# Putting VectorE's sums and low parts of the weights in program order, and moving two waits at the ends

## The chip, the cores and the metric

One core of a Trainium2 chip runs the whole kernel. The metric is the device time of one execution in microseconds (us), lower is better. Engines are named as in the profile: PE is TensorE, DVE VectorE, ACT ScalarE, POOL GpSimd, SP SyncE.

## The reference

One layer of a hybrid decoder trunk, in float32, for 256 tokens of width 2048:

```python
h = x + 0.5 * swiglu(rmsnorm(h, ffn1_norm), ffn1_w_gu, ffn1_w_down)       # D_FF = 5632
proj = rmsnorm(h, mix_norm) @ w_in
gu, gv, z, xbc, dt_raw = jnp.split(proj, split_at, axis=-1)
a_out = chunked_sgu(gelu(gu), gelu(gv), gm_v_norm, gm_w_s, gm_b_s)
m_out = mamba2_group(z, xbc, dt_raw, ssm_conv_w, ssm_conv_b, ssm_dt_bias, ssm_a_log, ssm_d, ssm_norm)
h = h + concatenate([a_out, m_out]) @ w_out
h = h + memory_cross_attention(rmsnorm(h, xa_norm), rmsnorm(mem, mem_norm), xa_w_q, xa_w_kv, xa_w_o)
h = h + 0.5 * swiglu(rmsnorm(h, ffn2_norm), ffn2_w_gu, ffn2_w_down)
return rmsnorm(h, final_norm)
```

Nearly all of the work is in the projections, whose weights are read once from memory.

## The kernel before

Each float32 matrix product is made of three products of parts: every operand is split into a high part in PE's fast float32 format and a low part, which is the rest, and PE adds high x high, high x low and low x high. A weight arrives as a raw block of 128 x 2048 elements (four pieces of 128 x 512; pool `wraw`, 3 buffers). ACT casts it to the high part (`high`, L161; `whigh`, 3 buffers) and DVE subtracts to get the low part (`low`, L166; `wlow`, 2 buffers).

In `proj_sum` there are two kinds of blocks, named by a letter in a string of kinds. A C block is used as it is: 24 matmuls. An S block serves a scheme that saves one of eight products by working on sums of the four pieces: `split_sums` has DVE make four sums in three instructions (L184 two at once, L185, L186), and then the high and low part of three raw pieces and of the four sums: 21 matmuls. The sums and their parts have one buffer each. Products m1, m6, m5 and m7 collect over all S blocks of a group and are read out after the last of them (`mid`), when that block's other products are still to come.

A feed-forward network runs over 11 chunks of 512 hidden columns (kinds CSCSCSCC each, numbered 0 to 10 here), and its down projection comes in two parts, after chunks 4 and 10. Between chunks, the finished hidden chunk is transposed by PE and split into operands: L339 and L340 for operands of C blocks, L410 to L422 (`forms`, `hids`) for those of S blocks. `part` instructions (L496, L523) read PE's results.

The order of instructions on PE is that of the program. On the other engines a scheduler sets the order when the kernel is built, from its own estimate of times. It keeps data dependencies, and it keeps one instruction behind another where the program says so with `behind` (L152). Each engine then runs its queue in that order. Before the change, the sums and low parts of weights are free of such ties, so a low part can stand between two sums or ahead of another block's.

At the end, each of the four column groups `h[0]` to `h[3]` is 128 x 512 for each of two token tiles (t = 0, 1). `finish` (L1016) has ACT square and sum them (L319, output `junk`), DVE and POOL make the reciprocal root (`rstd_of`: L325, L326, L327), and DVE (L1029) and ACT (L1031) scale and store.

## Time and profile before

| | |
|---|---|
| runs (3) | 2515.29, 2517.97 (median), 2519.0 us |
| profiled execution | 2517.8 us, its span 2516.1 us |
| granted PE clock, mean | 0.996 |
| PE busy | 98% of the span |
| DVE busy | 78% |
| ACT busy | 51% |
| POOL busy | 1% |
| memory traffic | 189 GB/s over the span |

A row of the timeline is: start in us, length in us, engine, line, operation, output and inputs, shape, how many in a row, and in brackets the idle time of the engine just before it and what ended that. A row of the windows gives a stretch, its length, busy time and number of instructions of PE, of PE's weight loads, of DVE, ACT and POOL, then the granted PE clock, the share of the DMA engines and GB/s. All times are from the start of the span.

### The profile page before, as it was taken

The page shows a single profiled execution, that of the slowest core. Times are in us where ns is not written, and L with a number is a line of the kernel's source. Part 1 is how long each engine was busy: PE and PEld are TensorE (multiplying, and loading weights), DVE is VectorE, ACT ScalarE, POOL GpSimd, SP SyncE. Part 2 cuts the span into 40 slices and gives each one's busy share as a digit, 9 for nine tenths or more (in the row PEclk, how much of TensorE's full clock was granted, in tenths as well). Part 3 has the DMA queues.
Part 4 walks back from the last instruction along what each step waited for, and adds up shares of the span by engine and source line. Part 5 has one row for each costly group of instructions (what it writes and reads, how often), then busy time and mean ns, then how long its engine had stood idle before and what let it go on. Part 6 is the DMA issues. An engine that isn't in the chain of part 4 may idle for free.

```text
span 2516.1 us, 31418 instructions
## 1 busy us (share of the span) xinstructions
PE 2478.2 (98%) x12673; PEld 2110.1 (84%) x12673; DVE 1951.9 (78%) x1830; ACT 1286.9 (51%) x1164; POOL 21.9 (1%) x46
## 2 busy tenths in 40 slices
PE   9999999999999999999999999999999999999997
PEld 7778888888789998788888999988877888888876
DVE  7888888898776678655688755678798888989876
ACT  6555445555446454435555544455555454555543
POOL 0000000000000000000000000000000000000000
PEclk9999999999999999999999999999999999999999
DMA  7555666555555555545556654555655566566553
GB/s 237 187 197 192 202 209 200 189 197 191 177 175 166 196 179 198 201 159 192 178 191 201 218 173 163 169 183 170 199 191 194 186 200 216 185 201 201 190 195 134
DMA packets 205762, 476.75 MB, mean 189 GB/s; under 512 B 15040, under 2 KB 17248, under 8 KB 204848
## 3 DMA queue, kind: packets, MB, share of 16 engines
q1 hardware_dynamic: 202800, 464.31, 56.1%
q0 software_dynamic: 1840, 9.26, 1.1%
q8 instruction: 99, 1.62, 0.3%
q10 hardware_dynamic: 976, 1.18, 0.1%
q14 instruction: 47, 0.39, 0.0%
HBM read 472.57 MB, written 2.13 MB: 189 GB/s over the span
## 4 chain that ended last, share of the span: by engine, by line
PE 69%; DVE 16%; issue 8%; ACT 4%; DMA 3%; SPq 0%; DVEq 0%; POOL 0%; ACTq 0%; POOLq 0%
PE acc L73 65%; DVE lo L166 8%; ACT hi L161 3%; DVE sum L184 2%; PE tpose L76 1%; DMA raw<-in_w_gu 1%; DVE sum L185 1%; DVE part L496 1%; DMA raw<-in_w_dn 1%; DVE sum L186 1%; PE yp L73 1%; DVE part L523 1%; DVE hids L422 0%; PE logits L73 0%; PE o L73 0%
## 5 line engine op out<-in xcount | busy, mean ns | idle before, releaser
L161 ACT CAST hi<-raw 128x2048 fp32r<-128x2048 f32 (+1 forms) x438 | 791.3, 1807 | 813.9 <-PE acc L73 657.6
L166 DVE TENSOR_TENSOR lo<-raw,hi 128x2048 fp32r<-128x2048 f32 (+1 forms) x438 | 943.6, 2155 | 256.4 <-PE acc L73 190.1
L73 PE MATMUL acc<-hi,xp_ffn 128*128 128x512 f32 x1824 | 577.7, 391 | 1.3 <-ACT hi L176 1.3
L73 PEld LDWEIGHTS acc<-hi,xp_ffn 128*128 128x128 f32 x1824 | 343.5, 188 | 73.1 <-ACT hi L176 2.1
L166 DVE TENSOR_TENSOR lo<-sum,hi 128x2048 fp32r<-128x2048 f32 x109 | 249.6, 2290 | 153.4 <-ACT hi L161 153.4
L73 PE MATMUL acc<-lo,xp_ffn 128*128 128x512 f32 x912 | 356.1, 390 | 0.0
L161 ACT CAST hi<-sum 128x2048 fp32r<-128x2048 f32 x109 | 208.3, 1911 | 210.7 <-DVE sum L186 198.1
L73 PE MATMUL acc<-hi,hid 128*128 128x512 f32 x896 | 282.9, 390 | 0.0
L73 PE MATMUL acc<-hi,xt_mix 128*128 128x512 f32 x768 | 241.9, 393 | 0.0
L73 PEld LDWEIGHTS acc<-lo,xp_ffn 128*128 128x128 f32 x912 | 171.8, 188 | 35.8 <-DVE lo L177 0.4
L73 PEld LDWEIGHTS acc<-hi,hid 128*128 128x128 f32 x896 | 168.3, 188 | 34.8
L73 PE MATMUL acc<-xt_mix,hi 128*128 128x256 f32 x1024 | 186.0, 284 | 0.0
L73 PE MATMUL acc<-lo,hid 128*128 128x512 f32 x448 | 174.5, 390 | 0.0
L73 PEld LDWEIGHTS acc<-hi,xt_mix 128*128 128x128 f32 x768 | 144.3, 188 | 30.3 <-issue 0.5
L496 DVE TENSOR_TENSOR part<-acc,part 128x512 f32<-128x512 f32 x240 | 159.7, 686 | 11.0 <-PE acc L73 3.9
L73 PEld LDWEIGHTS acc<-xt_mix,hi 128*128 128x128 f32 x1024 | 159.8, 192 | 0.3
L73 PE MATMUL acc<-hi,xp_ffn1s 128*128 128x512 f32 x466 | 151.2, 393 | 2.2 <-DVE xp_ffn L340 1.3
L73 PE MATMUL acc<-hi,xp_ffn2s 128*128 128x512 f32 x466 | 150.9, 393 | 1.6 <-DVE hid L340 1.3
L73 PE MATMUL acc<-lo,xt_mix 128*128 128x512 f32 x384 | 149.8, 390 | 0.1
L73 PE MATMUL acc<-xt_mix,lo 128*128 128x256 f32 x512 | 145.5, 284 | 0.7 <-DVE lo L166 0.7
L184 DVE TENSOR_TENSOR sum<-raw 128x1024 f32<-128x1024 f32 x109 | 133.1, 1222 | 8.7 <-DMA raw<-in_w_gu 6.0
L73 PE MATMUL acc<-hi,hids 128*128 128x512 f32 x392 | 130.1, 402 | 0.1
(281 smaller groups left out, 3418.1 us busy)
## 6 DMA issues: line engine op xcount, KB each, us to landing
raw<-in_w_gu SPq DMA_DIRECT2D x286, 512.0 KB, 4.0
raw<-in_w_in SPq DMA_DIRECT2D x80, 1024.0 KB, 5.1
raw<-in_w_dn SPq DMA_DIRECT2D x60, 1024.0 KB, 5.4
raw<-in_w_gu SPq DMA_DIRECT2D x132, 256.0 KB, 4.1
raw<-in_w_kv SPq DMA_DIRECT2D x28, 1024.0 KB, 5.3
raw<-in_w_out SPq DMA_DIRECT2D x21, 1024.0 KB, 5.6
raw<-in_w_q SPq DMA_DIRECT2D x16, 1024.0 KB, 5.2
raw<-in_w_dn SPq DMA_DIRECT2D x28, 512.0 KB, 4.1
```

The costliest lines, as they stand in the source:

```text
L73: return pe(nc.tensor.matmul(out, lhsT=lhsT, rhs=rhs, start=start, stop=stop))
L76: return pe(nc.tensor.transpose(out=out, in_=in_, identity=identity))
L161: nc.scalar.copy(out=t[:, :n], in_=x[:, :n])
L166: nc.vector.tensor_tensor(out=t[:, :n], in0=x[:, :n], in1=hi[:, :n].bitcast(F32), op=ALU.subtract)
L184: nc.vector.tensor_tensor(out=t[:, 0:2], in0=raw[:, 0:3:2], in1=raw[:, 3:4].broadcast_to([P, 2, NC]), op=ALU.add)
L185: nc.vector.tensor_tensor(out=t[:, 2], in0=t[:, 0], in1=raw[:, 2], op=ALU.add)
L186: nc.vector.tensor_tensor(out=t[:, 3], in0=t[:, 2], in1=raw[:, 1], op=ALU.add)
L496: nc.vector.tensor_tensor(out=out, in0=a, in1=b, op=op)
L523: nc.vector.scalar_tensor_tensor(out=g, in0=u, scalar=nrm.rstd[:, t:t + 1], in1=g, op0=ALU.mult, op1=ALU.mult)
```

## The change

Three parts. First, every sum and every low part of a weight goes through `split_op`, which ties it behind the one before it in the program: for an S block the three sums, the low part of the raw pieces, the low part of the sums, and then the next block. Second, the negation of a small constant row (`ex<-rowb`, which needs the load of `rowb`) is tied behind the instruction that makes `dt` in the middle of the kernel. Third, in `finish`, groups 2 and 3 of token tile 0 are multiplied by the final weight ahead (L1032 after the change), what is left of their scaling becomes a product with one scalar (L1048), and that is tied behind the last addition into `h[3]` of tile 1; the order of the four groups is written out anew.

```diff
+    last_split = []
+    def split_op(**kw):
+        with behind(last_split):
+            last_split[:] = [nc.vector.tensor_tensor(**kw).ins]
...
     def low(pool, x, hi, n):
         t = pool.tile([P, 2 * KP, NC], F32R, name="lo")
-        nc.vector.tensor_tensor(out=t[:, :n], in0=x[:, :n], in1=hi[:, :n].bitcast(F32), op=ALU.subtract)
+        split_op(out=t[:, :n], in0=x[:, :n], in1=hi[:, :n].bitcast(F32), op=ALU.subtract)
...
     def split_sums(raw):
         t = wsum.tile([P, 4, NC], F32, name="sum")
-        nc.vector.tensor_tensor(out=t[:, 0:2], in0=raw[:, 0:3:2], in1=raw[:, 3:4].broadcast_to([P, 2, NC]), op=ALU.add)
-        nc.vector.tensor_tensor(out=t[:, 2], in0=t[:, 0], in1=raw[:, 2], op=ALU.add)
-        nc.vector.tensor_tensor(out=t[:, 3], in0=t[:, 2], in1=raw[:, 1], op=ALU.add)
+        split_op(out=t[:, 0:2], in0=raw[:, 0:3:2], in1=raw[:, 3:4].broadcast_to([P, 2, NC]), op=ALU.add)
+        split_op(out=t[:, 2], in0=t[:, 0], in1=raw[:, 2], op=ALU.add)
+        split_op(out=t[:, 3], in0=t[:, 2], in1=raw[:, 1], op=ALU.add)
...
-            nc.vector.scalar_tensor_tensor(out=dt[:, t, :], in0=pdt[:, t, :HEADS], scalar=rstd[:, t:t + 1],
+            raw_ins = nc.vector.scalar_tensor_tensor(out=dt[:, t, :], in0=pdt[:, t, :HEADS], scalar=rstd[:, t:t + 1],
                                            in1=rowb[:, 0, :], op0=ALU.mult, op1=ALU.add)
...
-        nc.vector.tensor_scalar(out=ex[:, NT, :], in0=rowb[:, 1, :], scalar1=-1.0, scalar2=None, op0=ALU.mult)
+        with behind([raw_ins.ins]):
+            nc.vector.tensor_scalar(out=ex[:, NT, :], in0=rowb[:, 1, :], scalar1=-1.0, scalar2=None, op0=ALU.mult)
...
+    scale_first = []
+    def finish(n, t, added):
...
-        if n < 2:
+        if n < 2 or t == 0:
             nc.vector.tensor_tensor(out=h[n][:, t, :], in0=h[n][:, t, :], in1=fws[n], op=ALU.mult)
         if n < 3:
             return
+        if t:
+            with behind([added.ins]):
+                scale_first.pop()()
         r = rstd_of(ss_f[:, t:t + 1, :], f"f{t}")
-        for m in (3, 0, 2, 1):
+        def scale(m):
             o = h[m][:, t, :]
-            if m > 1:
+            if m < 2:
+                nc.scalar.mul(o, o, r)
+            elif t:
                 nc.vector.scalar_tensor_tensor(out=o, in0=o, scalar=r, in1=fws[m], op0=ALU.mult, op1=ALU.mult)
             else:
-                nc.scalar.mul(o, o, r)
+                nc.vector.tensor_scalar(out=o, in0=o, scalar1=r, scalar2=None, op0=ALU.mult)
             queue = nc.sync if m > 1 else nc.scalar if t else nc.gpsimd
             queue.dma_start(out=o_v[:, t, m * NC:(m + 1) * NC], in_=o)
+        for m in (0, 1):
+            if t:
+                scale(3 - m)
+            scale(m)
+        if not t:
+            scale_first.append(lambda: (scale(3), scale(2)))
```

The instructions of SP and POOL keep their order, and so do PE's. What moves is DVE's order, and a little of ACT's. Lines after the change are 7 higher in the stretch of `proj_sum` and the networks; all split operations of weights are recorded at L169.

DVE at the passage from chunk 2 to chunk 3 of the first network, before (the numbers tell buffers apart; sum_1229 belongs to the S block after the C block of lo_1171, hid_1217 to the hidden chunk just made):

```order
L496 TENSOR_TENSOR part_1081<-acc_944,part_1080 128x512
L184 TENSOR_TENSOR sum_1229<-raw_1225 128x1024
L185 TENSOR_TENSOR sum_1229<-sum_1229,raw_1225 128x512
L186 TENSOR_TENSOR sum_1229<-sum_1229,raw_1225 128x512
L166 TENSOR_TENSOR lo_1171<-raw_1166,hi_1169 128x2048
```

and further on, up to L340:

```order
L166 TENSOR_TENSOR lo_1235<-raw_1225,hi_1233 128x1536
L523 SCALAR_TENSOR_TENSOR part_1079<-part_1081,rstd_ffn1_440,part_1079 128x512
L184 TENSOR_TENSOR sum_1301<-raw_1297 128x1024
L166 TENSOR_TENSOR lo_1271<-raw_1266,hi_1269 128x2048
L417 TENSOR_TENSOR forms_1209<-forms_1207 128x256
L422 TENSOR_TENSOR hids_1201<-forms_1207,hids_1201 128x512
L418 TENSOR_TENSOR forms_1209<-forms_1207,forms_1209 128x128
L340 TENSOR_TENSOR hid_1217<-tpose_1218,hid_1217 128x2x256
```

The first of these places on DVE after the change:

```order
L503 TENSOR_TENSOR part_1081<-acc_944,part_1080 128x512
L169 TENSOR_TENSOR lo_1171<-raw_1166,hi_1169 128x2048
L503 TENSOR_TENSOR part_1078<-acc_859,part_1078 128x512
L169 TENSOR_TENSOR sum_1229<-raw_1225 128x1024
L503 TENSOR_TENSOR part_1080<-acc_866,part_1080 128x512
L503 TENSOR_TENSOR part_1079<-acc_873,part_1079 128x512
L530 SCALAR_TENSOR_TENSOR part_1078<-part_1080,rstd_ffn1_440,part_1078 128x512
L503 TENSOR_TENSOR part_1081<-acc_880,part_1081 128x512
L169 TENSOR_TENSOR sum_1229<-sum_1229,raw_1225 128x512
L530 SCALAR_TENSOR_TENSOR part_1079<-part_1081,rstd_ffn1_440,part_1079 128x512
L169 TENSOR_TENSOR sum_1229<-sum_1229,raw_1225 128x512
L169 TENSOR_TENSOR lo_1235<-raw_1225,hi_1233 128x1536
```

and, right behind that, up to the line that was L340 (now L347):

```order
L169 TENSOR_TENSOR lo_1239<-sum_1229,hi_1237 128x2048
L169 TENSOR_TENSOR lo_1271<-raw_1266,hi_1269 128x2048
L424 TENSOR_TENSOR forms_1209<-forms_1207 128x256
L429 TENSOR_TENSOR hids_1201<-forms_1207,hids_1201 128x512
L425 TENSOR_TENSOR forms_1209<-forms_1207,forms_1209 128x128
L347 TENSOR_TENSOR hid_1217<-tpose_1218,hid_1217 128x2x256
```

The three sums of the S block have moved from ahead of lo_1171 to behind it, and the first sum of the next S block (sum_1301) from ahead of lo_1271 to behind L347.

DVE at the last S block of the first down projection, before (its block is raw_4639; raw_4688 is the C block after it):

```order
L184 TENSOR_TENSOR sum_4643<-raw_4639 128x1024
L166 TENSOR_TENSOR lo_4649<-raw_4639,hi_4647 128x1536
L185 TENSOR_TENSOR sum_4643<-sum_4643,raw_4639 128x512
L186 TENSOR_TENSOR sum_4643<-sum_4643,raw_4639 128x512
L166 TENSOR_TENSOR lo_4692<-raw_4688,hi_4690 128x2048
L166 TENSOR_TENSOR lo_4653<-sum_4643,hi_4651 128x2048
```

and there after:

```order
L169 TENSOR_TENSOR sum_4643<-raw_4639 128x1024
L169 TENSOR_TENSOR sum_4643<-sum_4643,raw_4639 128x512 x2
L169 TENSOR_TENSOR lo_4649<-raw_4639,hi_4647 128x1536
L169 TENSOR_TENSOR lo_4653<-sum_4643,hi_4651 128x2048
L169 TENSOR_TENSOR lo_4692<-raw_4688,hi_4690 128x2048
```

The sums stand together, and the low part of the sums ahead of that of the next C block.

DVE at the end of the kernel after the change (h2 and h3 are the column groups, acc PE's results, fw the final weight):

```order
L464 SCALAR_TENSOR_TENSOR h2_92<-acc_18611,h2_92 128x512
L332 TENSOR_REDUCE ms_19000<-ss_f_14000 128x1
L1032 TENSOR_TENSOR h3_93<-h3_93,fw_18994 128x512
L333 TENSOR_SCALAR ms_19000<-ms_19000 128x1
L464 SCALAR_TENSOR_TENSOR h3_93<-acc_18618,h3_93 128x512
L1048 TENSOR_SCALAR h3_93<-h3_93,rstd_f0_18999 128x512
L1048 TENSOR_SCALAR h2_92<-h2_92,rstd_f0_18999 128x512
```

Before, the two scalings of h3 and h2 (L1029) stood right behind the line that is L333 now, ahead of the last addition into h3, and no product of h3 stood between the two steps of the reciprocal root.

## The prediction

> **What bounds the kernel now.** I read the page's first section, then what TensorE (PE) waited for, then the single waits in PE's timeline, the granted clock after them, and VectorE's (DVE) timeline ahead of each kind.

> ```profile
> span 2516.1 us, 31418 instructions
> PE 2478.2 (98%) x12673; PEld 2110.1 (84%) x12673; DVE 1951.9 (78%) x1830; ACT 1286.9 (51%) x1164; POOL 21.9 (1%) x46
> ...
> PE acc L73 <- DVE lo L166: 19.8, 19, 3.5
> PE acc L73 <- DVE hid L340: 2.2, 6, 0.7
> PE acc L73 <- DVE xp_ffn L340: 1.6, 2, 1.3
> ```

> PE is busy for 98% of the span, and its order is the same in both kernels. So the change can win only what PE waits, what PE loses at a lower clock, and the two ends of the span. Of the waits (us in total, times, longest), 19 for a low part are 19.8 us, and 8 for L340, which empties a transpose bank, are 3.8. The waits one by one (in brackets the idle time and what ended it):

> ```profile
> 68.44 0.50 PE L73 MATMUL acc<-hi,xp_ffn1s 128*128 128x512 f32 x1 [1.26 <-DVE xp_ffn L340]
> ...
> 88.19 0.51 PE L73 MATMUL acc<-lo,xp_ffn1s 128*128 128x512 f32 x1 [0.85 <-DVE lo L166]
> ...
> 157.06 0.50 PE L73 MATMUL acc<-hi,xp_ffn1s 128*128 128x512 f32 x1 [0.24 <-DVE hid L340]
> ...
> 643.08 0.79 PE L73 MATMUL acc<-lo,hids 128*128 128x512 f32 x1 [3.51 <-DVE lo L166]
> ...
> 1306.83 0.50 PE L73 MATMUL acc<-lo,mts 128*128 128x512 f32 x1 [1.50 <-DVE lo L166]
> ...
> 1392.75 0.50 PE L73 MATMUL acc<-lo,mts 128*128 128x512 f32 x1 [0.83 <-DVE lo L166]
> ...
> 2268.14 0.51 PE L73 MATMUL acc<-lo,xp_ffn2s 128*128 128x512 f32 x1 [0.48 <-DVE lo L166]
> ...
> 2483.84 0.51 PE L73 MATMUL acc<-lo,hids 128*128 128x512 f32 x1 [3.51 <-DVE lo L166]
> ```

> Four kinds. The down projection's last S block: three waits of 3.51 (643.08, 2415.63 and 2483.84). w_out: 1.50 and 0.83. The last S block of a feed-forward (FFN) chunk: eleven waits, the first 0.85 at 88.19, the last 0.48 at 2268.14, 6.2 together. The remaining three low-part waits, 0.7, lie in the down projections. L340's lie at the passage from one chunk to the next. A matmul that ends a wait lasts 0.50 and delays the next, so a wait costs about 0.15 more than its bracket.

> The clock after the waits (PE's busy time, its granted clock after "PEclk" at the end, as windows):

> ```profile
> 643.08:648.60 5.52, 5.52 (x13) 4.37 (x14) 3.63 (x6) 0.00 (x0) 0.00 (x0) 0.50 0.40 154
> 2416.71:2420.12 3.41, 3.41 (x10) 2.63 (x9) 2.62 (x5) 0.00 (x0) 0.00 (x0) 0.50 0.33 127
> 2484.97:2488.38 3.41, 3.41 (x10) 2.64 (x9) 2.65 (x5) 0.00 (x0) 0.00 (x0) 0.50 0.02 5
> 1308.30:1311.70 3.40, 3.40 (x16) 2.81 (x15) 3.40 (x5) 1.30 (x1) 0.00 (x0) 1.00 0.45 131
> ```

> After each wait of 3.51 PE runs at clock 0.50 for 5.5 or 3.4 us; after the wait of 1.50 it keeps 1.00. In 3.41 us 10 matmuls ran where 16 or 17 would have. The loss is between 10/17 kept (1.4, 1.4 and 2.3, so 5.1) and half (6.2); I take 5.7.

> **The change, part by part.**

> *Down projection.* DVE around the first long wait:

> ```profile
> 633.62 1.75 DVE L166 TENSOR_TENSOR lo<-raw,hi 128x1536 fp32r<-128x1536 f32 x1
> 635.29 0.69 DVE L185 TENSOR_TENSOR sum<-sum,raw 128x512 f32<-128x512 f32 x1
> 636.01 0.69 DVE L186 TENSOR_TENSOR sum<-sum,raw 128x512 f32<-128x512 f32 x1
> 638.53 2.29 DVE L166 TENSOR_TENSOR lo<-raw,hi 128x2048 fp32r<-128x2048 f32 x1 [1.82 <-PE acc L73]
> 640.74 2.29 DVE L166 TENSOR_TENSOR lo<-sum,hi 128x2048 fp32r<-128x2048 f32 x1
> ```

> Two things are late: the sums stand behind a low part (1.67 from start to start), and lo<-sum, which PE needs, stands behind the low part of the next C block, which itself waits for a buffer until 638.53. Chained, lo<-sum runs 2.2 earlier for the second reason and 1.7 for the first, so it ends about 3.9 before 643.03, ahead of the 639.5 at which PE runs dry. The low part put behind it is for the block after this one, a whole S block away, so it has cover. All three waits go (3 x (3.51 + 0.15) = 11.0), the slow clock with them (5.7), and the three small ones (0.7 + 0.45 = 1.1): -17.8. If only the order of the two low parts helped, 1.3 of each wait would stay.

> *w_out.* The same pair (the low part between L184 and L185) makes the two waits there: 1.50 + 0.83 + 0.3, -2.6.

> *Last S block of a chunk.* Here too lo<-sum moves ahead of a low part: 6.2 + 11 x 0.15, -7.9. *First passage of each FFN* (68.44 and its like in the second): L340 comes ahead of a 2.2-us low part, 1.6 + 0.3, -1.9.

> *The other passages between chunks* lose. The one near 141, for DVE, PE and ScalarE (ACT) in turn:

> ```profile
> 139.46 1.23 DVE L184 TENSOR_TENSOR sum<-raw 128x1024 f32<-128x1024 f32 x1 [0.50 <-DMA raw<-in_w_gu]
> ...
> 142.05 2.29 DVE L166 TENSOR_TENSOR lo<-raw,hi 128x2048 fp32r<-128x2048 f32 x1
> ...
> 151.84 1.23 DVE L184 TENSOR_TENSOR sum<-raw 128x1024 f32<-128x1024 f32 x1
> 152.98 2.29 DVE L166 TENSOR_TENSOR lo<-raw,hi 128x2048 fp32r<-128x2048 f32 x1
> ...
> 156.32 0.69 DVE L340 TENSOR_TENSOR hid<-tpose,hid 128x512 fp32r<-128x512 f32 x1
> ...
> 141.03 0.39 PE L73 MATMUL acc<-lo,xp_ffn 128*128 128x512 f32 x1
> ...
> 143.12 1.90 ACT L161 CAST hi<-sum 128x2048 fp32r<-128x2048 f32 x1
> ```

> The low part at 142.05 (lo_1171) writes one of two buffers, which PE leaves with its matmul of 141.03, so at about 141.5. Before, DVE used the time up to then for the block's sums, 139.46 to 142.05. Now lo_1171 stands first in the chain, so DVE waits for 141.5 with the sums queued behind it, and they are done in the stretch that leads to L340, which PE waits for at 157.06. From the end of L340 in before, 157.01: start 0.5 earlier; plus the three sums, 1.14 + 0.60 + 0.60 = 2.34 from start to start; less the next block's L184, which moves behind L340, 1.14; plus 0.4, because lo<-sum now follows its cast closely (cast 1.90 beside a low part of 1.67, and the hand-over). That is 158.1, or 1.1 later, on top of the 0.24 that PE waits there already. Eight passages in each FFN have this order (chunks 2 to 4 and 6 to 10). Where L340 was not waited for, it had little room; I price all sixteen alike, 16 x 1.08 = +17.3. Bounds: 0.4 each (the hand-over alone, the rest covered) and 2.2 (nothing credited for L184): +6 to +35. I take 1.08, since each addend is a duration of this trace. The waits become 1.1 to 1.6 us long, in the class of the 1.50 that kept the clock.

> [...]

> *Opening.* DVE, ACT and PE, and two windows:

> ```profile
> 7.68 0.18 DVE L652 TENSOR_SCALAR ex<-rowb 128x32 f32<-128x32 f32 x1 [6.45 <-DMA rowb<-in_rows]
> 7.78 0.48 DVE L346 SCALAR_TENSOR_TENSOR xp_ffn<-tpose,col,xp_ffn 128x256 fp32r<-128x256 f32 x1
> ...
> 6.30 0.47 ACT L345 ACTIVATE xp_ffn<-tpose,col 128x256 fp32r<-128x256 f32 x1 [2.48 <-PE tpose L76]
> ...
> 9.32 0.79 PE L73 MATMUL acc<-hi,xp_ffn 128*128 128x512 f32 x1 [1.35 <-ACT hi L176]
> ...
> 10.31:13.72 3.41, 3.41 (x9) 2.64 (x10) 1.49 (x3) 0.52 (x1) 0.00 (x0) 1.00 0.99 346
> 13.73:17.14 3.41, 3.41 (x19) 2.81 (x18) 1.06 (x3) 1.58 (x4) 0.00 (x0) 1.00 1.01 342
> ```

> Without L652 ahead, L346 can follow ACT's 6.30 + 0.47 at about 6.82 and not at 7.78; ACT's casts and the first matmul follow: -0.9. Bounds: 0 (the weight loads come late instead) and -2.6 (PE, which runs 9 matmuls in the window before 13.7 and 19 in the next, also comes to its full rate one window sooner: 1.7 more). The moved L652 is 0.18 in a stage where DVE has room: nothing.

> *End.* DVE, then ACT, then PE's last matmul:

> ```profile
> 2506.28 1.42 DVE L1029 SCALAR_TENSOR_TENSOR h<-h,rstd_f,fw 128x512 f32<-128x512 f32 x2 [0.69 <-POOL rstd_f L327]
> 2507.61 0.69 DVE L457 SCALAR_TENSOR_TENSOR h<-acc,h 128x512 f32<-128x512 f32 x1
> ...
> 2506.28 1.33 ACT L1031 ACTIVATE h<-h,rstd_f 128x512 f32<-128x512 f32 x2 [0.18 <-POOL rstd_f L327]
> 2508.33 0.63 ACT L319 ACTIVATE junk<-h 128x512 f32<-128x512 f32 x1 [0.71 <-DVE h L457]
> ...
> 2505.58 0.39 PE L73 MATMUL acc<-hi,hid 128*128 128x512 f32 x1
> ```

> PE's last matmul ends at about 2506.0, and the last addition (2507.61) need no longer wait behind two L1029. But one of the new products stands between L325 and L326, 0.6, so POOL's rstd is that much later, and so are ACT's two scalings, which stay ahead of the last junk: 2506.28 + 0.6 + 1.33 = 2508.2 against 2508.33. Of 1.6 on DVE 0.1 to 0.2 is left: -0.2, between 0 and -1.6.

> Sum: -17.8 - 2.6 - 7.9 - 1.9 + 17.3 - 0.9 - 0.2 = -14.0. The profiled execution took 2517.8 (1.7 beside its span), the median 2517.97, so 2503.8 by the one and 2504.0 by the other.

> **Rivals.**

> *The clock falls at the passages (slower).* Sixteen waits of 1.1 to 1.6 us each followed by 3.41 us at 0.50: 16 x 1.6 = +26, so 2530. For it: nothing here shows a wait between 1.50 and 3.51, and sixteen tries are many. Against: 1.26 and 1.50 without a fall. It decides once nine of sixteen fall.

> *The passages cost their upper bound.* 2.2 each, +35 in place of +17: 2522, within the noise. For it: from 142.05 to L340 every DVE instruction of the rows above follows without idle, so nothing absorbs a further delay, a late weight load for one. Against: the L184 moved behind L340 is seen in the order.

> *The passages cost nearly nothing.* 0.4 each: 2493. For it: PE waits for the banks only, and DVE has 22% of idle time. Against: none of that idle time lies behind lo_1171.

> *The chain doesn't cure the late low parts.* Raw buffers are released later by later low parts, the loads land later, and lo<-sum in the down projections stays late by 2 to 3 us: about 12 of the 17.8 don't come, 2516. For it: low parts of raw blocks now follow the sums. Against: the low part at 633.62 ran without idle, so neither its load nor its cast was late there.

> **How the numbers follow.** The forecast has 0.70; falling clock 0.09, dear passages 0.08, cheap passages 0.07, no cure 0.06. The forecast's own range is 2497 to 2512: opening and end -2.9 or +1.1, passages 0.7 to 1.5 each, the clock 5.1 to 6.2. The 8-in-10 range leaves out the falling clock and most of the dear passages: 2495 to 2515. 0.2% (5 us) is about what a measurement of this kernel tells from no change: the forecast and the cheap passages are faster than 2512.9, less a few cases at the forecast's edge (0.76); dear passages and no cure mostly within (0.14); the falling clock and a tail of the dear passages slower (0.10).

> **What would show it.** PE's three waits of 3.51 and the clock of 0.50 behind them gone. The eleven waits at 88.19 and its like gone. L340's successor as the longest of PE's waits: 16 times 1.0 to 1.6, in place of 8. DVE idle about 2.5 us for PE ahead of each chunk's first low part. First matmul near 8.4. The last axpy near 2506 less the gain, ACT's last junk hardly earlier. Wrong would be: clock 0.50 after the passages, waits there over 2 us, or a new DMA wait of PE.

## The result and the profile after

The changed kernel took 2500.44 us (median of four runs, 2499.35 to 2500.98), the kernel before 2518.48 beside it (four runs, 2515.29 to 2519.0): a ratio of 0.993, 95% interval 0.9913 to 0.9948, so 18 us or 0.7% faster by the medians (13 to 22 us by the interval); between the two profiled spans it is 16.9 us. The forecast was 2504.0, range 2495 to 2515.

The head of the page after, and then what PE waited for (us in total, times, longest):

```profile
span 2499.2 us, 31437 instructions
PE 2467.2 (99%) x12673; PEld 2104.5 (84%) x12673; DVE 1967.4 (79%) x1832; ACT 1291.7 (52%) x1164; POOL 20.6 (1%) x46
```

```profile
PE acc L73 <- DVE hid L347: 16.1, 16, 1.3
PE acc L73 <- DVE lo L169: 3.4, 9, 0.8
```

The waits for low parts fell from 19.8 to 3.4 us and those for L347 (L340 before) rose from 3.8 to 16.1. That goes most of the way to balance, so the waits alone don't explain 16.9 us: PE's busy time also fell, by 11 us, with as many matmuls. The clock is about 6 of these 11, as the windows of after show. At the places of the three 3.51-us waits PE now runs at clock 1.00 (the first three rows; in the first, 26 matmuls in 5.56 us against 13 in 5.52), and it keeps 1.00 behind a passage between chunks (the fourth):

```profile
641.04:646.60 5.56, 5.56 (x26) 4.62 (x25) 5.20 (x5) 3.61 (x3) 0.00 (x0) 1.00 0.64 228
2406.40:2409.80 3.40, 3.40 (x15) 2.83 (x16) 3.40 (x4) 0.99 (x2) 0.00 (x0) 1.00 0.14 31
2469.10:2472.50 3.40, 3.40 (x17) 2.82 (x16) 3.04 (x4) 1.71 (x3) 0.00 (x0) 1.00 0.05 16
156.20:159.60 3.40, 3.40 (x15) 2.83 (x16) 3.37 (x6) 1.06 (x3) 0.00 (x0) 1.00 0.75 286
```

PE issues the same matmuls in the same order in every kernel here, so the start of one can be set against its start in the kernel before. The difference, in us (positive is earlier), at the matmuls that started in the kernel before at the times of the head row, and in the last column the difference of the spans:

| kernel | 55 | 610 | 660 | 1200 | 1400 | 1830 | 2385 | 2500 | end |
|---|---|---|---|---|---|---|---|---|---|
| after | -0.5 | -1.7 | 4.7 | 5.6 | 8.8 | 8.8 | 5.5 | 16.6 | 16.9 |
| e1 | -0.1 | -1.1 | 5.4 | 6.4 | 9.5 | 9.5 | 6.3 | 18.1 | 18.5 |
| e3 | 0.6 | 0.4 | 6.9 | 7.4 | 8.1 | 8.1 | 8.2 | 19.7 | 19.7 |
| e9 | 0.1 | -1.0 | 0.2 | 0.5 | 3.7 | 3.7 | 0.7 | 1.3 | 1.7 |
| e8 | -0.4 | 8.0 | 14.5 | 15.3 | 18.4 | 18.4 | 24.9 | 36.7 | 37.1 |

For after, from column to column: opening -0.5; first network with its passages -1.2; the last part of its down projection +7.2 (6.5 of it by 660, the rest before w_in begins at 731); w_in +0.2; w_out +3.1; attention 0; second network -3.3 (0.2 of it already in its last down projection); the rest of the last down projection +11.1; the end +0.3. The gain is the down projections, 18.1; all the rest sums to -1.2.

DVE at the last S block of the first down projection, after:

```profile
634.32 1.42 DVE L169 TENSOR_TENSOR sum<-sum,raw 128x512 f32<-128x512 f32 x2
635.66 1.75 DVE L169 TENSOR_TENSOR lo<-raw,hi 128x1536 fp32r<-128x1536 f32 x1
637.81 2.29 DVE L169 TENSOR_TENSOR lo<-sum,hi 128x2048 fp32r<-128x2048 f32 x1 [0.40 <-ACT hi L161]
640.11 2.29 DVE L169 TENSOR_TENSOR lo<-raw,hi 128x2048 fp32r<-128x2048 f32 x1
```

lo<-sum ends at 640.1, 2.9 earlier than before although PE reaches the place 1.6 later, and PE doesn't wait. The low part of the next block, now behind it, is in time too. At the second of the three places a short wait stayed:

```profile
2406.39 0.50 PE L73 MATMUL acc<-lo,hids 128*128 128x512 f32 x1 [0.52 <-DVE lo L169]
```

There the cast of the sums stood on ACT behind the cast of another block, which waited 3.89 us for its load.

DVE at the passage from chunk 2 to 3, after, and PE's waits at two passages:

```profile
139.53 2.29 DVE L169 TENSOR_TENSOR lo<-raw,hi 128x2048 fp32r<-128x2048 f32 x1 [2.69 <-issue]
...
142.34 1.22 DVE L169 TENSOR_TENSOR sum<-raw 128x1024 f32<-128x1024 f32 x1
...
149.87 2.29 DVE L169 TENSOR_TENSOR lo<-sum,hi 128x2048 fp32r<-128x2048 f32 x1 [0.32 <-ACT hi L161]
...
155.42 0.68 DVE L347 TENSOR_TENSOR hid<-tpose,hid 128x512 fp32r<-128x512 f32 x1
```

```profile
156.16 0.50 PE L73 MATMUL acc<-hi,xp_ffn1s 128*128 128x512 f32 x1 [1.32 <-DVE hid L347]
...
390.09 0.50 PE L73 MATMUL acc<-hi,xp_ffn1s 128*128 128x512 f32 x1 [0.86 <-DVE hid L347]
```

The 2.69 us idle ahead of the low part is the time in which the kernel before made the sums; they now stand inside the stretch that ends with L347. (The bracket names no releaser; a matmul that ends at 139.44, just ahead of 139.53, is the one that the prediction names as leaving the buffer.) With 0.32 more for the cast this is the mechanism forecast.

### The profile page after: what moved, and what is told of

Read it like the earlier page. It is cut to its first block, busy times and chain, and to the rows that moved or that the text cites. A ratio compares the mean times of both kernels' runs of the same rounds, so it can differ in the third digit from the quotient of the medians.

```text
span 2499.2 us, 31437 instructions
## 1 busy us (share of the span) xinstructions
PE 2467.2 (99%) x12673; PEld 2104.5 (84%) x12673; DVE 1967.4 (79%) x1832; ACT 1291.7 (52%) x1164; POOL 20.6 (1%) x46
## 4 chain that ended last, share of the span: by engine, by line
PE 81%; DVE 9%; issue 7%; ACT 2%; DMA 1%; SPq 0%; DVEq 0%; POOL 0%; POOLq 0%; ACTq 0%
PE acc L73 77%; DVE lo L169 3%; ACT hi L161 2%; DVE part L503 2%; DVE sum L169 1%; PE tpose L76 1%; DVE part L530 1%; PE yp L73 1%; PE logits L73 0%; PE o L73 0%; DVE hid L347 0%; DVE cacc L622 0%; DMA raw<-in_w_dn 0%; DMA raw<-in_w_gu 0%; PE mixed L73 0%
## 5 line engine op out<-in xcount | busy, mean ns | idle before, releaser
L161 ACT CAST hi<-raw 128x2048 fp32r<-128x2048 f32 (+1 forms) x438 | 791.3, 1807 | 865.0 <-PE acc L73 726.9
L169 DVE TENSOR_TENSOR lo<-raw,hi 128x2048 fp32r<-128x2048 f32 (+2 forms) x446 | 949.3, 2130 | 327.5 <-PE acc L73 223.3
L73 PE MATMUL acc<-hi,xp_ffn 128*128 128x512 f32 x1824 | 576.0, 390 | 0.4 <-ACT hi L183 0.4
L73 PEld LDWEIGHTS acc<-hi,xp_ffn 128*128 128x128 f32 x1824 | 342.4, 188 | 72.1 <-ACT hi L183 1.1
L73 PE MATMUL acc<-lo,xp_ffn 128*128 128x512 f32 x912 | 355.2, 389 | 0.4 <-DVE lo L169 0.4
L169 DVE TENSOR_TENSOR lo<-sum,hi 128x2048 fp32r<-128x2048 f32 x109 | 249.8, 2292 | 45.3 <-ACT hi L161 45.3
L73 PE MATMUL acc<-hi,hid 128*128 128x512 f32 x896 | 282.6, 390 | 0.0
L161 ACT CAST hi<-sum 128x2048 fp32r<-128x2048 f32 x109 | 208.8, 1915 | 93.2 <-DVE sum L169 75.9
L73 PE MATMUL acc<-hi,xt_mix 128*128 128x512 f32 x768 | 241.7, 393 | 0.0
L73 PEld LDWEIGHTS acc<-lo,xp_ffn 128*128 128x128 f32 x912 | 171.3, 188 | 36.7 <-DVE lo L169 1.4
L73 PEld LDWEIGHTS acc<-hi,hid 128*128 128x128 f32 x896 | 168.2, 188 | 34.7
L73 PE MATMUL acc<-xt_mix,hi 128*128 128x256 f32 x1024 | 186.0, 284 | 0.0
L73 PE MATMUL acc<-lo,hid 128*128 128x512 f32 x448 | 174.5, 390 | 0.0
L73 PEld LDWEIGHTS acc<-hi,xt_mix 128*128 128x128 f32 x768 | 144.2, 188 | 30.3 <-issue 0.5
L73 PEld LDWEIGHTS acc<-xt_mix,hi 128*128 128x128 f32 x1024 | 159.6, 192 | 0.3
L73 PE MATMUL acc<-hi,xp_ffn1s 128*128 128x512 f32 x466 | 151.6, 393 | 8.0 <-DVE hid L347 8.0
L73 PE MATMUL acc<-hi,xp_ffn2s 128*128 128x512 f32 x466 | 151.6, 393 | 8.0 <-DVE hid L347 8.0
L169 DVE TENSOR_TENSOR sum<-sum,raw 128x512 f32<-128x512 f32 x218 | 150.4, 690 | 5.2
L73 PE MATMUL acc<-lo,xt_mix 128*128 128x512 f32 x384 | 149.7, 390 | 0.0
L73 PE MATMUL acc<-xt_mix,lo 128*128 128x256 f32 x512 | 145.2, 284 | 0.7 <-DVE lo L169 0.7
L169 DVE TENSOR_TENSOR sum<-raw 128x1024 f32<-128x1024 f32 x109 | 132.7, 1217 | 0.0
```

Source lines behind the costliest of these rows:

```text
L73: return pe(nc.tensor.matmul(out, lhsT=lhsT, rhs=rhs, start=start, stop=stop))
L161: nc.scalar.copy(out=t[:, :n], in_=x[:, :n])
L169: last_split[:] = [nc.vector.tensor_tensor(**kw).ins]
```

## The experiments

The kernels differ from the changed kernel by the lines shown; e3 also has the opening and the end of the kernel before. Differences in us are between medians. The median of the kernel before, run beside each group, lay between 2516.6 and 2518.5, and the intervals of the ratios are 2 to 4 us to either side. So a difference of a microsecond, as in e1 and e2, is read from the traces, each of one execution, and not from the medians.

**e1, the opening alone undone.**

```diff
-        with behind([raw_ins.ins]):
-            nc.vector.tensor_scalar(out=ex[:, NT, :], in0=rowb[:, 1, :], ...)
+        nc.vector.tensor_scalar(out=ex[:, NT, :], in0=rowb[:, 1, :], ...)
```

> The changed kernel without its second part: the negation ex<-rowb is free again, as before. Theory A (the opening is bound by the weight loads; starting 0.9 us earlier and reaching the full clock 3.4 us earlier is given back by 50 us in waits of PE for low parts whose raw blocks land late): the time of the changed kernel, 2500.4 us, within 0.5, first matmul back near 9.3, and the gain over the kernel before at the matmul near 49 us no worse than the -0.4 us of the changed kernel. Theory B (the opening brings what the prediction priced, 0.9 us, or 2.5 with the clock): 2501.3 to 2502.9.

Measured: 2500.28 (five runs), ratio to before 0.9933 (0.9921 to 0.9946). Nothing is seen to be lost without the earlier start, as theory A has it. In the table's column 55 the kernels with the earlier start (after, e9, e8) stand at -0.5 to 0.1, those without it (e1, e3) at -0.1 and 0.6. The traces show how it is given back. ACT, after and then e1:

```profile
23.86 1.91 ACT L161 CAST hi<-raw 128x2048 fp32r<-128x2048 f32 x1 [4.07 <-DMA raw<-in_w_gu]
```

```profile
23.31 1.90 ACT L161 CAST hi<-raw 128x2048 fp32r<-128x2048 f32 x1 [2.08 <-DMA raw<-in_w_gu]
```

PE, after:

```profile
28.91 0.50 PE L73 MATMUL acc<-lo,xp_ffn 128*128 128x512 f32 x1 [0.20 <-DVE lo L169]
...
35.73 0.50 PE L73 MATMUL acc<-lo,xp_ffn1s 128*128 128x512 f32 x1 [0.59 <-DVE lo L169]
...
42.21 0.50 PE L73 MATMUL acc<-lo,xp_ffn1s 128*128 128x512 f32 x1 [0.76 <-DVE lo L169]
...
49.08 0.50 PE L73 MATMUL acc<-lo,xp_ffn1s 128*128 128x512 f32 x1 [0.46 <-DVE lo L169]
```

PE started at 8.45 and reached its full rate one window sooner (19 matmuls from 10.31 to 13.72, against 9 in the kernel before; the granted clock in the profile reads 1.00 for both), so that it was 2.5 us ahead of the kernel before by 14. But the cast of a later block waits for its load until 23.86 (23.31 in e1) although PE is ahead; from there ACT and DVE are late and PE waits four times. The loads run no faster for it. The same stretch before and after, with the share of the DMA engines and the GB/s at the end of the row:

```profile
6.90:24.00 17.10, 15.75 (x64) 11.93 (x62) 10.10 (x16) 8.79 (x15) 0.00 (x0) 1.00 1.03 364
6.90:24.00 17.10, 16.49 (x77) 12.72 (x77) 10.10 (x15) 8.45 (x15) 0.00 (x0) 1.00 1.03 361
```

**e2, the end alone undone** (the `finish` of the kernel before).

> The changed kernel with the end of the kernel before (two scalings ahead of the last addition). Theory A (ScalarE sets the end; moving DVE's scalings frees little): 0.3 to 0.5 us slower than the changed kernel, 2500.8. Theory B (DVE's two scalings set the end, 1.6 us): 2502.0.

Measured: 2501.21 (five runs, 2501.07 to 2501.39), 0.8 slower than the changed kernel; the two profiled spans are equal, 2499.2, with PE's last matmul 0.3 earlier in e2. Between the theories, nearer to A: the part brings 0.3 by the traces and 0.8 by the medians, not 1.6. DVE and ACT at the end of the changed kernel:

```profile
2488.77 0.68 DVE L1032 TENSOR_TENSOR h<-h,fw 128x512 f32<-128x512 f32 x1
2489.36 0.14 DVE L333 TENSOR_SCALAR ms<-ms 128x1 f32<-128x1 f32 x1
2489.45 0.69 DVE L464 SCALAR_TENSOR_TENSOR h<-acc,h 128x512 f32<-128x512 f32 x1
...
2490.20 1.33 ACT L1044 ACTIVATE h<-h,rstd_f 128x512 f32<-128x512 f32 x2 [0.66 <-POOL rstd_f L334]
2491.44 0.61 ACT L326 ACTIVATE junk<-h 128x512 f32<-128x512 f32 x1
```

The last addition follows PE at once, as meant. The product at 2488.77 delays L333 and so POOL and ACT, whose two scalings run until the last junk starts: 2.0 after PE's end, where it was 2.4 before.

**e3, the chain in the down projections alone**, with the opening and the end of the kernel before:

```diff
+        if not tied[0]:
+            last_split.clear()
         with behind(last_split):
...
+            tied[0] = True
             add_sum(w_dn, c_from * NC, hts, ...)
+            tied[0] = False
```

> The kernel before with the chain of sums and low parts tied only inside the two down projections; gate-up, w_in, w_out, attention, opening and end as before. Theory A (three waits of 3.5 us, small ones and the slow clock behind them are 17.2 us, counted matmul by matmul): 17.2 us faster than before, 2501.1, as fast as the whole change; no wait over 0.7 us in the down projections, clock 1.00 throughout after 14 us; the sixteen passages between chunks wait as before (0.2 to 0.7). Theory B (the gain is spread over chunk ends and w_out, and the down projection brings only the waits, not the clock): 2507 or more.

Measured: 2499.72 (five runs), 17.1 below the kernel before beside it (2516.8), ratio 0.9931 (0.9918 to 0.9945). Theory A. This part alone is worth the whole change. What PE waits for in it:

```profile
PE acc L73 <- DVE lo L171: 8.9, 17, 1.5
PE acc L73 <- DVE hid L349: 1.9, 5, 0.5
```

Set against 19.8 in 19 waits before, 10.9 us of waits have gone; the remaining 6 us are about what the clock cost: e3's granted clock is 0.999 over the span of its profile, against 0.996 in the kernel before.

**e9, the chain everywhere but in the down projections:**

```diff
+        if free[0]:
+            last_split.clear()
         with behind(last_split):
...
+            free[0] = True
             add_sum(w_dn, c_from * NC, hts, ...)
+            free[0] = False
```

> The changed kernel with the chain opened inside the two down projections alone, so that their order is the scheduler's again. Theory A (the whole change's gain is the down projections' 17 us; what the chain wins at chunk ends, first passages and w_out, 12.6, is lost again at the passages, 15.0, and the ends bring nothing): 2516.5 to 2518, no change against the kernel before; three waits of 3.5 us and clock 0.50 behind them. Theory B (the parts depend on each other, and the chain elsewhere also cures part of the down projections): 2505 to 2512.

Measured: 2517.03 (eleven runs) against 2516.56, ratio 1.0001 (0.9992 to 1.001). Theory A: no change. Its waits:

```profile
PE acc L73 <- DVE hid L349: 15.9, 16, 1.3
PE acc L73 <- DVE lo L171: 12.8, 9, 3.5
```

Its longest wait is 3.5 us again, and its granted clock 0.997 over the span of its profile, where the changed kernel has 0.999. With e3 this settles the division: the parts add up, and outside the down projections gains and losses nearly cancel.

**e4, sums free to run ahead of a waiting low part:**

```diff
-            last_split[:] = [nc.vector.tensor_tensor(**kw).ins]
+        with behind(lows[-1:] + sums[-1:]):
+            lows.append(nc.vector.tensor_tensor(**kw).ins)
+    def sum_op(**kw):
+        with behind(lows[-2:-1] + sums[-1:]):
+            sums.append(nc.vector.tensor_tensor(**kw).ins)
```

> The changed kernel, but the three sums of an S block are tied only to each other and behind the low part before the last one, so that they may run ahead of the preceding C block's low part; low parts stay chained, and the low part of the raw pieces still follows the sums. In the order built from it the sums run ahead of the first low part at each passage, as in the kernel before, and in the down projections lo<-sum still precedes the next C block's low part. Theory A (the passages cost 15 us because the sums moved behind the wait for a buffer): 2485.4 us, PE's waits at the passages back to the 0.2 to 0.7 of before, no new waits elsewhere. Theory B (the passages cost because low parts are chained at all, or what is saved there is lost at late low parts): 2495 to 2501.

Measured: 2489.02 (four runs), 11.4 below the changed kernel, ratio to before 0.9888 (0.9874 to 0.9901). Mostly theory A: the passages' loss is the place of the sums. It stays 3.6 above the number, since free sums also took other places:

```profile
PE acc L73 <- DVE hid L351: 3.6, 8, 0.5
PE acc L73 <- DVE lo L169: 3.4, 6, 1.5
PE acc L73 <- DVE xp_ffn L351: 1.6, 2, 1.3
```

The first passage of each network waits again (1.6), as before, and near 42 us PE waits 1.5 for a low part that stood behind sums.

**e5, only the first S block's sums free, from chunk 2 on:**

```diff
-        with behind(lows[-2:-1] + sums[-1:]):
+        with behind((lows[-2:-1] if ahead[0] else lows[-1:]) + sums[-1:]):
...
+                ahead[0] = early and m == 1
                 parts = split_sums(raw)
+                ahead[0] = False
```

> The changed kernel with one loosening: from chunk 2 on, the sums of a chunk's first S block may run ahead of the low part before them (as in the kernel before); every other sum and all low parts are tied in program order. Theory A (the passages cost 15.0 us, counted at the matmuls that wait; e4 stayed 3.6 us above its expectation because its sums were free elsewhere too: 0.8 us more lost near 42 us, 1.9 at the two first passages, 0.8 in w_in): 2485.4 us, the two first passages without a wait as in the changed kernel, the other passages at 0 to 0.5. Theory B (e4's shortfall comes with the passages themselves, for example late loads once the sums run early): 2489 as e4.

Measured: 2489.71 (four runs), ratio 0.9889 (0.9873 to 0.9906). A miss by 4.3: the time is theory B's, but the traces don't show its late loads at the passages. The first passages are cured and eight others wait for nothing, but the eight that lead to operands of S blocks wait about 1.0 each:

```profile
PE acc L73 <- DVE hid L353: 7.9, 8, 1.0
```

DVE there shows that the scheduler put the next S block's first sum, 1.22 long, among the instructions that lead to L353 (the old L340):

```profile
152.16 0.43 DVE L430 TENSOR_TENSOR forms<-forms 128x256 f32<-128x256 f32 x1
152.50 1.22 DVE L173 TENSOR_TENSOR sum<-raw 128x1024 f32<-128x1024 f32 x1
153.64 0.28 DVE L431 TENSOR_TENSOR forms<-forms 128x128 f32<-128x128 f32 x1
...
154.65 0.68 DVE L353 TENSOR_TENSOR hid<-tpose,hid 128x512 fp32r<-128x512 f32 x1
```

**e8, e5 with the second S block's sums tied behind that instruction:**

```diff
-        with behind((lows[-2:-1] if ahead[0] else lows[-1:]) + sums[-1:]):
+        with behind((lows[-2:-1] if ahead[0] else lows[-1:] + (emptied[-1:] if second[0] else [])) + sums[-1:]):
...
+            emptied.append(lo.ins)
```

> e5 with one more tie: from chunk 2 on, the sums of a chunk's second S block run behind L347, as in the changed kernel, and no longer just ahead of it. Theory A (what e5 kept at eight passages, 7.9 us of waits and about 0.15 more each, is the 1.14-us sum that the scheduler put between the instructions that lead to L347): the eight waits of 1.0 shrink to 0 to 0.2, 2481 us. Theory B (they come from ACT's casts and from PE arriving earlier, so L347 moves but PE waits for the next thing): 2486 to 2490.

Measured: 2481.46 (four runs, 2480.7 to 2481.77), ratio 0.9858 (0.9845 to 0.9872), 35 us below before and 19 below the changed kernel: theory A. L353 is gone from PE's waits, and with it the 2.2 us that the kernel before waited at these passages, so that more comes back than the change had lost there:

```profile
PE acc L73 <- DVE lo L169: 2.6, 7, 0.7
PE idle L73 <- DVE idle L568: 1.3, 1, 1.3
```

**e6 and e7, the waits at the passages made longer** by doing L347's subtraction three and five times, to see what length costs the clock:

```diff
-            lo = nc.vector.tensor_tensor(out=dst[:, q:q + 2, S:], in0=ps, ...)
+            for again in range(3):      # 5 in e7
+                lo = nc.vector.tensor_tensor(out=dst[:, q:q + 2, S:], in0=ps, ...)
```

> The changed kernel with the subtraction that empties a transpose bank (L347) done three times in place of once, with the same result, so that each of the sixteen waits at the passages grows by 1.2 us, from 0.9 or 1.3 to 2.1 or 2.5. Theory A (PE's clock holds over waits of this length): 16 x 1.2 = 19 us more, 2520, granted clock 1.00 behind the passages. Theory B (the clock falls for 3.4 us after such waits): up to 26 us more than that, 2530 to 2546, with 0.50 in the windows behind the passages.

> The same with the subtraction done five times: the sixteen waits grow by 2.4 us, to 3.3 or 3.7. Theory A (the clock falls only after waits of about 3.5 us, as in the kernel before): 38 us for the waits, 2539, and about 1.6 for each of the seven waits of 3.7 us, 2550. Theory B (the clock is not sensitive to these waits, and fell in the down projections for another reason): 2539. Theory C (it falls after all sixteen): 2565.

Measured, in one execution each: 2568.41 and 2639.12. Both are far above every theory. At some passages two banks are emptied in a row, so the repetitions count twice (in e6 six subtractions, 3.67 us, at 454.89), and at others the scheduler put other work between them. In e6 the sixteen waits are 60.2 us in all, up to 4.5, not 2.5, and in e7 97.7, up to 6.9. So the numbers expected don't tell the theories apart, but the clock behind waits of many lengths can be read. The sixteen waits of after (up to 1.32) kept 1.00, and so did one of 1.91 in e6 (it ended at 552.87; 1.00 from 552.90 to 556.30). In e6 three waits of 3.33 to 3.35 did not act alike: behind those that ended at 458.11 and 2209.25 PE kept 1.00, behind the one that ended at 410.54 it ran at 0.50. And e7 has one of 2.24 (ended at 278.29) with 0.50 behind it. A matmul that ends a wait of 3.34 in e6, and one of 3.35:

```profile
2209.25 0.47 PE L73 MATMUL acc<-hi,xp_ffn2s 128*128 128x512 f32 x1 [3.34 <-DVE hid L348]
...
410.54 0.47 PE L73 MATMUL acc<-hi,xp_ffn1s 128*128 128x512 f32 x1 [3.35 <-DVE hid L348]
```

and windows of 3.41 us on one grid, the one with the wait's end and the next. The grid is counted from 412.00, where the low stretch begins (the last one, at 2210.83, lies 1798.83 us behind it, 527 times 3.4133):

```profile
2207.41:2210.82 3.41, 1.57 (x7) 1.35 (x8) 3.41 (x5) 1.08 (x1) 0.00 (x0) 1.00 0.86 297
2210.83:2214.24 3.41, 3.41 (x17) 2.83 (x16) 3.05 (x3) 1.85 (x1) 0.00 (x0) 1.00 0.02 5
...
408.58:411.99 3.41, 1.45 (x7) 1.24 (x8) 3.41 (x6) 1.30 (x1) 0.00 (x0) 1.00 0.92 304
412.00:415.41 3.41, 3.41 (x10) 2.67 (x9) 3.17 (x4) 1.43 (x1) 0.00 (x0) 0.50 0.01 2
```

Waits of one length; PE was busy for 1.57 us of the first window and kept the clock, for 1.45 of the third and lost it. In these rows the busy time in a window of the grid told the two apart, and not the length of the wait (the last section has the windows of the kernel before). In e7, a wait of 2.24 that lay inside one window:

```profile
275.70:279.11 3.41, 1.17 (x6) 0.68 (x5) 3.41 (x3) 1.90 (x1) 0.00 (x0) 1.00 0.00 0
279.12:282.52 3.40, 3.40 (x10) 2.66 (x9) 3.33 (x4) 0.00 (x0) 0.00 (x0) 0.50 0.23 63
```

## Why the prediction was right, step by step

The measured steps below are read from the start differences of PE's matmuls, from the second matmul ahead of a place to the fifth behind it, or over a whole stretch.

- *Down projection*, -17.8 forecast: -18.1 measured, -17.1 by e3's medians. The terms agree less well than the sum. The three waits brought 10.5 (11.0 forecast), as 0.52 of the second stayed, and the clock 5.9 (5.7). The 1.1 for three small waits was a misreading: they are not in the down projections but in w_in (operand xt_mix), and they are still there. The page's row for them, with their 0.7 us of waiting near its end, before and then after:

```profile
L73 PE MATMUL acc<-xt_mix,lo 128*128 128x256 f32 x512 | 145.5, 284 | 0.7 <-DVE lo L166 0.7
L73 PE MATMUL acc<-xt_mix,lo 128*128 128x256 f32 x512 | 145.2, 284 | 0.7 <-DVE lo L169 0.7
```

  What came in place of that 1.1 was 1.7 from pauses in the down projections too short for the list of waits (0.4 at 2402.96, for one), which the prediction did not price. That the step comes so near is in part luck. At the first wait lo<-sum was forecast 3.9 earlier and came 2.9 earlier, at 640.1: DVE reached the block's sums 0.6 later, as PE was late too, and the cast took 0.4. The cure doesn't hang on PE's being late: in e3, where PE is 0.4 ahead of the kernel before there, lo<-sum ends at 637.9 and PE doesn't wait.
- *w_out*, -2.6: -2.9. *Chunk ends*, -7.9: -9.5 at the eleven. *First passages*, -1.9: -2.2. All three were priced too small by one term: a wait was taken to cost 0.15 beyond its bracket, and at the eleven chunk ends it cost 0.30, since the matmul behind is late as well.
- *Other passages*, +17.3: +15.9 at the sixteen (15.0 in the expectations of e5 and e9, which count the waiting matmul alone). The mechanism and 1.08 were right for most (0.95 to 1.16 in eleven; 1.28 and 1.31 after chunk 7; 0.64 once in the second network), and pricing all alike was off where L340 had room: 0.47 at two.
- *Opening*, -0.9 forecast: +0.5 in the table, and nothing seen to be lost without it (e1). This is the step whose mechanism failed. Its lower bound, "0 (the weight loads come late instead)", was the case; the value taken priced the earlier start alone. The row that showed it was in the trace before: ACT's cast at 23.30 waited 2.18 us for a load.
- *End*, -0.2: -0.3 in the spans, up to -0.8 by e2's medians.
- The sum came out at -14.0 against -16.9 between the spans and -18 between the medians. Of the 2.9, chunk ends give 1.6, passages 1.4, down projections, w_out and the first passages 0.3 each, w_in (not in the sum) 0.2 and the end 0.1; the opening takes 1.4 back.
- *Rivals.* The clock didn't fall at the passages, the passages were neither dear nor free, and lo<-sum was late only once, by 0.5. With sixteen waits of up to 1.32 us the changed kernel has no stretch at 0.50 from 8.46 to 2493.36, and in windows of 3.41 us counted from 8.46 PE was busy for 2.09 us or more of each that lies between 20 us and the end of its last matmul. The windows at full clock that rows of the kernel before, e6 and e7 show to be followed by 0.50 had 1.45 or less.

## What to carry to other kernels

A strict program order on a helper engine is as good as its worst wait: an instruction that waits for a buffer holds up all that is tied behind it, also work that was ready (2.69 us at a passage). Tie only the pairs that a trace shows in the wrong order (e3 has the whole gain with the down projections alone tied), leave free what can fill the wait (e4), and then look at what the scheduler did with the freedom (e5, e8). Price a wait of the bottleneck engine with the clock behind it: curing three waits of 3.5 us brought 10.5 in waits and 5.9 in clock. And look up where a small wait lies before it goes into a sum.
